# A hybrid decoder layer on one core: the arithmetic of GpSimd given to VectorE, and eight one-hot comparisons written as one

## The chip, the core and the metric

One NeuronCore of a Trainium2 chip runs the whole kernel. The metric is device time in microseconds (us) of one execution; the kernel before takes 2576.43 us, the median of 3 runs (2575.58 to 2576.53). The program has one instruction queue for each engine: TensorE (PE in the profile; its weight loads are PEld), VectorE (DVE), ScalarE (ACT), GpSimd (POOL) and SyncE (SP), which issues nearly all DMAs. Each queue runs in order; semaphores order the queues against each other.

## The reference: what is computed

The input x is 256 tokens of 2048 features. One layer does, all in float32:

```
h  = RMSNorm(x);  P = h @ W_in                       # 6152 columns, split among two groups of heads
mLSTM group (4 heads of 256): causal conv, q/k, gates, chunkwise matrix memory, norm, output gate
dilated group (8 heads of 128): rotary q/k, three dilated windows merged, norm
x += concat(groups) @ W_out
x += CrossAttention(RMSNorm(x), RMSNorm(mem))        # 4 heads of 512, 256 memory tokens
x += PEER(RMSNorm(x))
out = RMSNorm(x)
```

PEER holds 16384 experts, each one row of `u_tab` and one row of `v_tab`. Per token and for each of 8 heads, a query scores 128 first keys and 128 second keys; the best 16 of each make 256 sums, of which the best 16 are picked, with a softmax over them as gates. The result is the sum over the picks of gate * gelu(u . x) * v.

## The kernel before, in words

**Weights.** Activations stand with features on the 128 partitions and the 256 tokens along the free dimension. All big products go through 400 weight tiles of 128x2048 float32 (1 MB each). A tile is loaded by SP (`wload`, line 97) into one of 3 buffers `wst`. `wsplit` (lines 103 to 113) then makes, for each of its two halves of 1024 columns, a high part `whi` by a cast on ScalarE (line 111) and a low part `wlo = wst - whi` by one subtraction (line 112); 3 buffers of halves hold each. `lin_a` (line 122) goes over the 16 chunks of the contraction: per chunk one matmul of `whi` with 512 columns (line 126; high and low part of the activations side by side) and one of `wlo` with 256 columns (line 127).

**Who subtracts.** The argument `lo_engine` of `wsplit` names the engine of line 112. VectorE has it by default. With "both" the half used last goes to GpSimd (32 tiles of the projections: `w_aqk`, `w_min`, `w_mo`). With `G` both halves go to GpSimd: the 16 tiles of `w_pq` (line 688) and the first 32 of the 128 tiles of `uT` (`u_block`, line 626, called in lines 732 and 781). That makes 128 of 800 halves on GpSimd.

**Other work on GpSimd.** The sums of squares of the norms (`square_into`, line 198: ScalarE squares, GpSimd adds 128x256), eight multiplications with a triangle (line 420), and three of the last sixteen multiplications of the output (line 870).

**The part of the program around the change.** After the output product of the cross attention (tiles of `w_xo`) come:

1. 16 tiles of `w_pq`, two for each PEER head. `pq` (line 692) joins the two halves of a product; a small product with the keys (line 669) gives scores in PSUM, and `top16` (lines 658 to 662) takes the best 16 of 128 in five VectorE operations, for two halves of the tokens. After a head's second tile, `cand` (line 677, one broadcast addition) and another `top16` over 256 follow. Beside them runs `scaled_input`: the norm `rstd_ffn`, then `xs` (line 645) and the parts of `hsc` (line 163), the moving operand of all `uT` tiles.
2. The first `u_block`s. Beside them runs `select_chain`: on VectorE, sixteen times, two operations `eq` over 128x512 (lines 709 and 711) and a reduction (line 713); PE then transposes the result into `selT` (line 727).
3. The other `u_block`s up to the 32nd, with 32 gate groups of 8 tokens between them (`gate_group`, line 740). For each token two one-hot rows are made on VectorE: `ob` (line 748) compares the 128 key numbers `iota` with the token's picked second keys, `oa` (line 749) with the first keys, times the gates. PE multiplies them (line 755), ScalarE copies the result out of PSUM (line 758), and a DMA writes it to DRAM. `oa` and `ob` have 2 buffers each.
4. Four more `u_block`s, and then 128 tiles of `v` (lines 818 and 819) with the last 92 tiles of `uT` between them. These cannot start before all gates are in DRAM, because `coef_half` reads them back by expert.

**What sets the order.** The functions above are generators that yield, and `tick` takes one step of each between two tiles of weights. The framework's scheduler then places the instructions on each queue by its own estimates of their durations and by free buffers; a queue runs what it was given in that order.

Of the kernel before, what the change touches and what calls it, by code (L numbers as in the profile page):

```python
# [20 lines left out]
P = 128  # L21
# [18 lines left out]
# columns of the packed small parameters  # L40
S_GMIX, S_GCROSS, S_GMEM, S_GFFN, S_GFIN = 0, 16, 32, 48, 64
S_CW, S_CB, S_GM, S_GA, S_BI, S_BF, S_N = 80, 112, 120, 128, 136, 137, 138
# columns of the packed constants
# [5 lines left out]
def hybrid_layer(ctx: ExitStack, tc: tile.TileContext, a, out):  # L49
    nc = tc.nc  # L50
    V, S, G, PE = nc.vector, nc.scalar, nc.gpsimd, nc.tensor
# [48 lines left out]
    def wtile(src, lo_engine=None, order=(0, 1)):  # L100
        return wsplit(wload(src), lo_engine, order)

    def wsplit(st, lo_engine=None, order=(0, 1)):
        """the parts of the tile's two halves; lo_engine "both" gives the half used last to GpSimd"""
        parts = {}
        for i in order:
            hi = wp.tile([P, 1024], F32R, tag="whi", name=f"whi{n_w[0]}_{i}", bufs=3)
            lo = wp.tile([P, 1024], F32R, tag="wlo", name=f"wlo{n_w[0]}_{i}", bufs=3)
            eng = (V, G)[i != order[0]] if lo_engine == "both" else lo_engine or V
            src = st[:, i * 1024:(i + 1) * 1024]  # L110
            S.copy(hi, src)  # L111
            eng.tensor_tensor(lo, src, hi.bitcast(F32), op=OP.subtract)  # L112
            parts[i] = hi, lo

        def part(which):
            return lambda at, n=P: parts[at // 1024][which][:, at % 1024:at % 1024 + n]
        return part(0), part(1)
# [4 lines left out]
    def lin_a(ps, hi, lo, mov, kcs=range(KC)):  # L122
        """ps[:, :256] + ps[:, 256:] = W.T @ h; mov(k) holds both parts of h's chunk."""
# [6 lines left out]
    def lin_b(pss2, kg, hi, lo, h):  # L130
        """pss2[tt] += h[:, tt].T @ W for four chunks of the contraction."""
# [10 lines left out]
    def rstd_of(dst, ss, n):  # L142
        """dst = (ss / n + eps) ** -0.5: a first guess from the exponent's bits, three steps of Newton's method"""
# [11 lines left out]
    def split_scaled(dst, k, src, g):  # L155
        """dst[:, k] = both parts of src * g (g per partition)"""
# [15 lines left out]
    def as_column(row, name):  # L172
        """[P, 256] with equal partitions -> [P, 2], tokens on partitions."""
# [8 lines left out]
    def residual_block(pool, ps, n, g_at, acc, nxt, first):  # L182
        """resid += ps; acc += resid ** 2; nxt = both parts of resid * g"""
# [8 lines left out]
    def square_into(pool, acc, x, first, tag):  # L192
        if first:
            S.activation(acc, x, AF.Square)
        else:
            sq = pool.tile([P, T], F32, tag="rsq", name=f"rsq{tag}", bufs=2)
            S.activation(sq, x, AF.Square)  # L197
            G.tensor_tensor(acc, acc, sq, op=OP.add)  # L198

    # ================= projections and the two head groups =================  # L200
    chains = []

    def tick():
        """the next step of every chain of small work, between two tiles of weights"""
# [16 lines left out]
    with tc.tile_pool(name="ph1", bufs=2) as p1:  # L221
# [9 lines left out]
        hm = lambda k: h[:, k, :]  # noqa: E731  # L231
# [17 lines left out]
        def join(dst, ps, tag):  # L249
            """dst = ps[:, :256] + ps[:, 256:]"""  # L250
# [4 lines left out]
        def head_norm(sq_parts, n, name):  # L255
            """rstd over the head's features, on every partition"""
# [9 lines left out]
        def proj_rows(src, dst):  # L266
            """one group of 512 columns, tokens on partitions: dst [P, 2, 512]"""
# [15 lines left out]
        def start_chain():  # L283
# [14 lines left out]
            # log sigmoid(f) = min(f, 0) - ln(1 + exp(-|f|))  # L298
# [67 lines left out]
        for half in range(2):  # L366
            vrow = p1.tile([P, 2, 512], F32, tag="vrow", name=f"av{half}")
            proj_rows(a["w_av"][half], vrow)
            for hh in range(4):
                hd = 4 * half + hh  # L370
                qs = p1.tile([P, 2, T], F32, tag="c32", name=f"qs_{hd}")
                for w in range(2):
                    ps = mm_tile()
                    lin_a(ps, *wtile(a["w_aqk"][2 * hd + w], "both"), hm)
# [6 lines left out]
        rows, ogs = {}, {}  # L381

        def mlstm_in(hd):
            """causal conv on the head's two blocks of channels"""
# [4 lines left out]
            for j in range(2):  # L389
                blk = 2 * hd + j  # L390
                ps = mm_tile()
                lin_a(ps, *wtile(a["w_min"][blk], "both"), hm)
# [13 lines left out]
        def mlstm_chain(hd, c32, wq):  # L406
# [4 lines left out]
            # decay weights exp(a_s - max_t), keys on partitions  # L411
# [4 lines left out]
            for s in range(2):  # L416
# [3 lines left out]
                G.tensor_tensor(dw[:, s, s * P:(s + 1) * P], dw[:, s, s * P:(s + 1) * P], tri, op=OP.mult)  # L420
            yield
            # q, k: [features, tokens]
# [23 lines left out]
            # denominator, on every partition  # L446
# [29 lines left out]
        def output_gate(hd):  # L476
            og = p1.tile([P, 2, T], F32, tag="og", name=f"og_{hd}")
            for j in range(2):
                ps = mm_tile()
                lin_a(ps, *wtile(a["w_mo"][2 * hd + j], "both"), hm)  # L480
# [17 lines left out]
    # ================= cross attention =================  # L498
    with tc.tile_pool(name="ph2", bufs=1) as p2:
# [18 lines left out]
        mm_ = lambda k: mh[:, k, :]  # noqa: E731  # L518
# [10 lines left out]
        cm = lambda k: cat[:, k, :]  # noqa: E731  # L529
        for n in range(KC):  # L530
            ps = mm_tile()
            lin_a(ps, *wtile(a["w_out"][n], None, (1, 0)), cm, list(range(8, KC)) + list(range(8)))
# [52 lines left out]
        xm = lambda k: hc[:, k, :]  # noqa: E731  # L585
# [24 lines left out]
        om = lambda k: ocat[:, k, :]  # noqa: E731  # L610
# [7 lines left out]
    # ================= PEER =================  # L618
    gdram = drp.tile([T // GT, P, NK * GT], F32, name="gdram")
    with tc.tile_pool(name="ph3", bufs=2) as p3:  # L620
        act = p3.tile([P, RING, T], F32, name="act", bufs=1)
        hpm = lambda k: hp[:, k, :]  # noqa: E731
        hs = big("hsc")

        def u_block(b, eng=None):
            ps = mm_tile()
            lin_a(ps, *wtile(a["uT"][b], eng), lambda k: hs[:, k, :])
# [6 lines left out]
        with tc.tile_pool(name="ph3g", bufs=2) as pg:  # L634
            def scaled_input():
                """the normalised input of the experts"""
# [45 lines left out]
            for hd in range(RH):  # L682
                keys = pg.tile([P, 2, NK], F32, tag="keys", name=f"keys{hd}")
                nc.sync.dma_start(keys, a["keysT"][:, 2 * hd:2 * hd + 2, :])
                for pp in range(2):
                    n = 2 * hd + pp
                    ps = mm_tile()
                    lin_a(ps, *wtile(a["w_pq"][n], G), hpm)
# [7 lines left out]
            def select_chain():  # L696
                """keys and gates of the picks, picks on partitions"""
# [34 lines left out]
            while chains:  # L732
                u_block(n_u, G)
# [3 lines left out]
        with tc.tile_pool(name="ph3h", bufs=2) as pg:  # L737
            gst = [None]

            def gate_group(t0):  # L740
                """gates of 8 tokens, [second key, first key] each, into gdram"""
# [3 lines left out]
                ob = pg.tile([P, 8, P], F32, tag="ob", name=f"ob{t0}")  # L745
                for i in range(8):
                    t = t0 + i
                    V.tensor_scalar(ob[:, i, :], iota, selT[:, 1, t:t + 1], None, op0=OP.is_equal)  # L748
# [31 lines left out]
            for b in range(n_u, 2 * EB):  # L780
                u_block(b, G)
# [179 lines left out]
```

## Time and profile before

| | |
|---|---|
| median of the runs | 2576.43 us |
| the profiled execution: first to last instruction (span) | 2554.4 us |
| around the span (median less span) | 22.0 us |
| `w_pq` tiles on PE | from 862.5 us |
| first one-hot row on VectorE | 1073.8 us |
| gate products on PE | 1079.3 to 1292.4 us |
| first matmul of `v` | 1316.3 us |

The profile is of one execution. For each engine it gives busy time, groups of like instructions with their number and mean duration, and the idle time before them with what ended it. A duration on VectorE or PE can reach into the next instruction's, because the engines are pipelined; what an instruction really holds the engine for is read from start to start in the timeline. "Granted clock" (PEclk) is the share of TensorE's full speed that was granted.

### The profile page before, as it was taken

The page shows a single profiled execution, that of the slowest core. Times are in us where ns is not written, and L with a number is a line of the kernel's source. Part 1 is how long each engine was busy: PE and PEld are TensorE (multiplying, and loading weights), DVE is VectorE, ACT ScalarE, POOL GpSimd, SP SyncE. Part 2 cuts the span into 40 slices and gives each one's busy share as a digit, 9 for nine tenths or more (in the row PEclk, how much of TensorE's full clock was granted, in tenths as well). Part 3 has the DMA queues.
Part 4 walks back from the last instruction along what each step waited for, and adds up shares of the span by engine and source line. Part 5 has one row for each costly group of instructions (what it writes and reads, how often), then busy time and mean ns, then how long its engine had stood idle before and what let it go on. Part 6 is the DMA issues. An engine that isn't in the chain of part 4 may idle for free.

```text
span 2554.4 us, 34778 instructions
## 1 busy us (share of the span) xinstructions
PE 2436.9 (95%) x13610; PEld 2117.2 (83%) x13610; DVE 1724.6 (68%) x2818; ACT 1202.1 (47%) x1649; POOL 401.6 (16%) x214
## 2 busy tenths in 40 slices
PE   7989999999999879788899999999999999999997
PEld 6777788888888768677888888888888888888886
DVE  6877758744456699899975555655655655556565
ACT  6555446444445434355554444444444444444343
POOL 3131313100001457545400000000000000000001
PEclk9999999999999989899999999999999999999998
DMA  6344435544544434344485656555655565555553
GB/s 244 140 144 148 139 125 205 191 168 173 175 176 169 166 119 162 128 167 184 183 289 213 211 188 208 204 194 202 209 203 184 212 212 200 197 184 183 196 198 116
DMA packets 98710, 466.78 MB, mean 183 GB/s; under 512 B 7537, under 2 KB 41585, under 8 KB 45297
## 3 DMA queue, kind: packets, MB, share of 16 engines
q1 hardware_dynamic: 96096, 447.71, 49.4%
q10 hardware_dynamic: 2448, 16.85, 1.6%
q8 instruction: 107, 1.75, 0.3%
q14 instruction: 59, 0.48, 0.1%
HBM read 445.65 MB, written 18.87 MB: 182 GB/s over the span
## 4 chain that ended last, share of the span: by engine, by line
PE 50%; DVE 14%; issue 1%; POOL 0%; DMA 0%; ACT 0%; DVEq 0%; POOLq 0%; SPq 0%; ACTq 0%
PE sm L818 16%; PE mm L126 15%; PE sm L819 8%; PE mm L127 8%; DVE ob L748 4%; DVE oa L749 4%; PE mm L818 2%; PE mm L819 1%; DVE cand L677 1%; DVE xs L645 0%; POOL wlo L112 0%; DVE hsc L163 0%; DVE eq L711 0%; DVE ut L630 0%; DVE eq L709 0%
## 5 line engine op out<-in xcount | busy, mean ns | idle before, releaser
L112 DVE TENSOR_TENSOR wlo<-wst,whi 128x1024 fp32r<-128x1024 f32 x672 | 825.5, 1230 | 692.0 <-ACT whi L111 689.3
L111 ACT CAST whi<-wst 128x1024 fp32r<-128x1024 f32 x800 | 834.2, 1049 | 937.5 <-PE mm L126 531.0
L126 PE MATMUL mm<-hsc,whi 128*128 128x512 f32 x2048 | 734.2, 400 | 4.1 <-ACT whi L111 4.1
L818 PE MATMUL sm<-coef,whi 128*128 128x512 f32 x1792 | 624.7, 391 | 0.0
L127 PE MATMUL mm<-hsc,wlo 128*128 128x256 f32 x2048 | 581.4, 284 | 9.9 <-POOL wlo L112 8.4
L819 PE MATMUL sm<-coef,wlo 128*128 128x256 f32 x1792 | 500.6, 280 | 0.0
L126 PEld LDWEIGHTS mm<-hsc,whi 128*128 128x128 f32 x2048 | 391.5, 191 | 91.5 <-ACT whi L111 5.0
L127 PEld LDWEIGHTS mm<-hsc,wlo 128*128 128x128 f32 x2048 | 395.1, 193 | 12.2 <-POOL wlo L112 10.3
L818 PEld LDWEIGHTS sm<-coef,whi 128*128 128x128 f32 x1792 | 335.2, 187 | 74.0
L112 POOL TENSOR_TENSOR wlo<-wst,whi 128x1024 fp32r<-128x1024 f32 x128 | 315.6, 2473 | 403.0 <-ACT whi L111 382.3
L819 PEld LDWEIGHTS sm<-coef,wlo 128*128 128x128 f32 x1792 | 338.3, 189 | 0.1
L198 POOL TENSOR_TENSOR facc<-facc,rsqf 128x256 f32<-128x256 f32 x11 | 11.9, 1084 | 1224.2 <-ACT rsqf L197 1224.0
L126 PE MATMUL mm<-h,whi 128*128 128x512 f32 x512 | 187.0, 407 | 0.0
L631 ACT ACTIVATE act<-ut 128x256 f32<-128x256 f32 x128 | 53.6, 419 | 216.3 <-DVE ut L630 216.3
L127 PE MATMUL mm<-h,wlo 128*128 128x256 f32 x512 | 145.4, 284 | 4.3 <-DVE wlo L112 4.0
L748 DVE TENSOR_SCALAR ob<-con,selT 128x128 f32<-128x128 f32 x256 | 127.1, 496 | 6.8 <-PE sm L727 6.8
L749 DVE TENSOR_SCALAR oa<-con,selT 128x128 f32<-128x128 f32 x256 | 119.4, 466 | 0.0
L126 PEld LDWEIGHTS mm<-h,whi 128*128 128x128 f32 x512 | 97.8, 191 | 22.8 <-issue 0.3
L198 POOL TENSOR_TENSOR acc<-acc,rsqr 128x256 f32<-128x256 f32 x30 | 39.2, 1308 | 430.1 <-ACT rsqr L197 425.5
L127 PEld LDWEIGHTS mm<-h,wlo 128*128 128x128 f32 x512 | 98.4, 192 | 6.8 <-DVE wlo L112 5.3
L126 PE MATMUL mm<-hp,whi 128*128 128x512 f32 x256 | 97.6, 420 | 3.3 <-DVE hp L158 3.3
L126 PE MATMUL mm<-ocat,whi 128*128 128x512 f32 x256 | 90.5, 399 | 0.0
(309 smaller groups left out, 3375.6 us busy)
## 6 DMA issues: line engine op xcount, KB each, us to landing
wst<-in_uT SPq DMA_DIRECT2D x128, 1024.0 KB, 4.8
wst<-in_v SPq DMA_DIRECT2D x128, 1024.0 KB, 4.8
wst<-in_w_aqk SPq DMA_DIRECT2D x16, 1024.0 KB, 4.8
wst<-in_w_out SPq DMA_DIRECT2D x16, 1024.0 KB, 4.8
wst<-in_w_xk SPq DMA_DIRECT2D x16, 1024.0 KB, 4.8
wst<-in_w_xq SPq DMA_DIRECT2D x16, 1024.0 KB, 4.8
wst<-in_w_xv SPq DMA_DIRECT2D x16, 1024.0 KB, 4.8
wst<-in_w_xo SPq DMA_DIRECT2D x16, 1024.0 KB, 4.8
```

The lines of the kernel that those rows point to most:

```text
L111: S.copy(hi, src)
L112: eng.tensor_tensor(lo, src, hi.bitcast(F32), op=OP.subtract)
L126: PE.matmul(ps, hi(k * P), mov(k), start=(n == 0), stop=False)
L127: PE.matmul(ps[:, 256:], lo(k * P), mov(k)[:, :256], start=False, stop=(n == len(kcs) - 1))
L198: G.tensor_tensor(acc, acc, sq, op=OP.add)
L631: S.activation(act[:, b % RING, :], tmp, AF.Gelu)
L677: V.tensor_tensor(cand, ts[:, tt, hd, 0, :, None].to_broadcast([P, TK, TK]), ts[:, tt, hd, 1, None, :].to_broadcast([P, TK, TK]), op=OP.add)
L748: V.tensor_scalar(ob[:, i, :], iota, selT[:, 1, t:t + 1], None, op0=OP.is_equal)
L749: V.tensor_scalar(oa[:, i, :], iota, selT[:, 0, t:t + 1], selT[:, 2, t:t + 1], op0=OP.is_equal, op1=OP.mult)
L818: PE.matmul(ps, hi(at), coef[:, c, :], start=(c == 0), stop=False)
L819: PE.matmul(ps[:, 256:], lo(at), coef[:, c, :256], start=False, stop=(c == EB - 1))
```

## The change

`G` is gone from the kernel. Line 112 is always on VectorE, so are the additions of line 198, the triangle and the last multiplications. In `gate_group`, the eight comparisons for `ob` are one VectorE instruction over 128x1024, in which both operands are broadcast; the eight for `oa` stay. The comments and docstrings are gone too, so that line numbers in the new kernel are lower by one between lines 110 and 744.

```diff
-    V, S, G, PE = nc.vector, nc.scalar, nc.gpsimd, nc.tensor
+    V, S, PE = nc.vector, nc.scalar, nc.tensor
...
-    def wsplit(st, lo_engine=None, order=(0, 1)):
+    def wsplit(st, order=(0, 1)):
...
-            eng = (V, G)[i != order[0]] if lo_engine == "both" else lo_engine or V
             src = st[:, i * 1024:(i + 1) * 1024]
             S.copy(hi, src)
-            eng.tensor_tensor(lo, src, hi.bitcast(F32), op=OP.subtract)
+            V.tensor_tensor(lo, src, hi.bitcast(F32), op=OP.subtract)
...
             S.activation(sq, x, AF.Square)
-            G.tensor_tensor(acc, acc, sq, op=OP.add)
+            V.tensor_tensor(acc, acc, sq, op=OP.add)
...
-                    lin_a(ps, *wtile(a["w_aqk"][2 * hd + w], "both"), hm)
+                    lin_a(ps, *wtile(a["w_aqk"][2 * hd + w]), hm)
...
-                G.tensor_tensor(dw[:, s, s * P:(s + 1) * P], dw[:, s, s * P:(s + 1) * P], tri, op=OP.mult)
+                V.tensor_tensor(dw[:, s, s * P:(s + 1) * P], dw[:, s, s * P:(s + 1) * P], tri, op=OP.mult)
...
-                    lin_a(ps, *wtile(a["w_pq"][n], G), hpm)
+                    lin_a(ps, *wtile(a["w_pq"][n]), hpm)
...
-                u_block(n_u, G)
+                u_block(n_u)
...
                 ob = pg.tile([P, 8, P], F32, tag="ob", name=f"ob{t0}")
+                V.tensor_tensor(ob, iota[:, None, :].to_broadcast([P, 8, P]),
+                                selT[:, 1, t0:t0 + 8, None].to_broadcast([P, 8, P]), op=OP.is_equal)
                 for i in range(8):
                     t = t0 + i
-                    V.tensor_scalar(ob[:, i, :], iota, selT[:, 1, t:t + 1], None, op0=OP.is_equal)
                     V.tensor_scalar(oa[:, i, :], iota, selT[:, 0, t:t + 1], selT[:, 2, t:t + 1],
                                     op0=OP.is_equal, op1=OP.mult)
...
-                        (G if i == 3 else V).tensor_tensor(o[:, i, :], resid[:, k, :], fin, op=OP.mult)
+                        V.tensor_tensor(o[:, i, :], resid[:, k, :], fin, op=OP.mult)
```

The two calls with "both" for `w_min` and `w_mo`, and the second call of `u_block` with `G`, change in the same way. How the instructions stand on the queues, before and now, is shown at three places.

The first is VectorE's queue in part 1 above, from the joining of the third `w_pq` product (`pq2`) on. Before:

```order
L692 TENSOR_TENSOR pq2_7360<-mm229_7317,pqt2_7361 128x256
L179 COPY col_ffn_7367<-sm230_7364 128x1 x2
L658 MAX ts_7181<-sm231_7370 128x8
L163 TENSOR_TENSOR hsc_7176<-xs0_7448,hsc_7176 128x256
L659 MAX_INDEX ti_7182<-ts_7181,sm231_7370 128x8
```

Now, at the same place (`wlo133` is the low part of the fourth `w_pq` tile, `_0` and `_1` its halves):

```order
L111 TENSOR_TENSOR wlo133_0_7405<-wst133_7402,whi133_0_7404 128x1024
L691 TENSOR_TENSOR pq2_7360<-mm229_7317,pqt2_7361 128x256
L178 COPY col_ffn_7367<-sm230_7364 128x1 x2
L657 MAX ts_7181<-sm231_7370 128x8
L111 TENSOR_TENSOR wlo133_1_7409<-wst133_7402,whi133_1_7408 128x1024
L658 MAX_INDEX ti_7182<-ts_7181,sm231_7370 128x8
```

The two subtractions of a `w_pq` tile stand between the picks now; the next tile's two (`wlo134`) come 39 rows further on, behind a head's picks and four rows each of `xs` and `hsc`.

The second is VectorE's queue in part 3, around the joining `ut18` of the 19th `u_block`. Before:

```order
L748 TENSOR_SCALAR ob96_9785<-con_74,selT_7177 128x128
L749 TENSOR_SCALAR oa96_9784<-con_74,selT_7177 128x128
L630 TENSOR_TENSOR ut18_9766<-mm301_9723,ut18_9766 128x256
L748 TENSOR_SCALAR ob104_9803<-con_74,selT_7177 128x128
L749 TENSOR_SCALAR oa104_9802<-con_74,selT_7177 128x128
```

Now (`ob104` is the group of 8 tokens from token 104 on; `wlo166` belongs to the 21st `u_block`, two tiles on from the one that `ut18` joins):

```order
L111 TENSOR_TENSOR wlo165_1_9742<-wst165_9735,whi165_1_9741 128x1024
L111 TENSOR_TENSOR wlo166_0_9810<-wst166_9807,whi166_0_9809 128x1024
L629 TENSOR_TENSOR ut18_9682<-mm301_9639,ut18_9682 128x256
L745 TENSOR_TENSOR ob104_9712<-con_74,selT_7177 128x1024
L749 TENSOR_SCALAR oa104_9711<-con_74,selT_7177 128x128 x8
L745 TENSOR_TENSOR ob112_9796<-con_74,selT_7177 128x1024
L749 TENSOR_SCALAR oa112_9795<-con_74,selT_7177 128x128 x8
L111 TENSOR_TENSOR wlo166_1_9814<-wst166_9807,whi166_1_9813 128x1024
```

A group takes nine instructions in place of sixteen, and the low parts stand in the same queue, one and a half to two tiles ahead of their use.

The third is PE's queue where the gate products begin. Before, they stand behind the last matmul of the 11th `u_block` (`whi156`):

```order
L126 MATMUL mm271_8988<-hsc_7176,whi156_1_8995 128x512
L127 MATMUL mm271_8988<-hsc_7176,wlo156_1_8996 128x256
L755 MATMUL sm272_9072<-oa0_9036,ob0_9037 128x128 x4
L755 MATMUL sm273_9078<-oa0_9036,ob0_9037 128x128 x4
L126 MATMUL mm274_9084<-hsc_7176,whi157_0_9087 128x512
```

Now they stand in the middle of the second half of the 12th:

```order
L126 MATMUL mm274_9070<-hsc_7176,wlo157_1_9078 128x256
L125 MATMUL mm274_9070<-hsc_7176,whi157_1_9077 128x512
L755 MATMUL sm272_9058<-oa0_9036,ob0_9037 128x128 x4
L755 MATMUL sm273_9064<-oa0_9036,ob0_9037 128x128 x4
L126 MATMUL mm274_9070<-hsc_7176,wlo157_1_9078 128x256
```

So about one and a half `u_block`s more stand ahead of the first gate product than before, and as many fewer behind it.

More of the change, by code (lines that the diff above doesn't have):

```diff
@@ L98, in wload, with wtile @@
         return st
-    def wtile(src, lo_engine=None, order=(0, 1)):
-        return wsplit(wload(src), lo_engine, order)
-    def wsplit(st, lo_engine=None, order=(0, 1)):
+    def wtile(src, order=(0, 1)):
+        return wsplit(wload(src), order)
+    def wsplit(st, order=(0, 1)):
         parts = {}
@@ L391, in mlstm_in @@
                 ps = mm_tile()
-                lin_a(ps, *wtile(a["w_min"][blk], "both"), hm)
+                lin_a(ps, *wtile(a["w_min"][blk]), hm)
                 xin = p1.tile([P, T + 3], F32, tag="xin", name=f"xin_{blk}")
@@ L479, in output_gate @@
                 ps = mm_tile()
-                lin_a(ps, *wtile(a["w_mo"][2 * hd + j], "both"), hm)
+                lin_a(ps, *wtile(a["w_mo"][2 * hd + j]), hm)
                 join(og[:, j, :], ps, f"o{hd}{j}")
@@ L531, in hybrid_layer @@
             ps = mm_tile()
-            lin_a(ps, *wtile(a["w_out"][n], None, (1, 0)), cm, list(range(8, KC)) + list(range(8)))
+            lin_a(ps, *wtile(a["w_out"][n], (1, 0)), cm, list(range(8, KC)) + list(range(8)))
             residual_block(p2, ps, n, S_GCROSS, acc, hc, n == 0)
@@ L623, in hybrid_layer, with u_block @@
         hs = big("hsc")
-        def u_block(b, eng=None):
+        def u_block(b):
             ps = mm_tile()
-            lin_a(ps, *wtile(a["uT"][b], eng), lambda k: hs[:, k, :])
+            lin_a(ps, *wtile(a["uT"][b]), lambda k: hs[:, k, :])
             tmp = p3.tile([P, T], F32, tag="ut", name=f"ut{b}")
@@ L780, in hybrid_layer @@
             for b in range(n_u, 2 * EB):
-                u_block(b, G)
+                u_block(b)
                 while n_g < (b + 1 - g0) * 32 // (2 * EB - g0):
```

## The prediction

> **What bounds the kernel now.** First the page: the span, and the engines' shares.
>
> ```profile
> span 2554.4 us, 34778 instructions
> PE 2436.9 (95%) x13610; PEld 2117.2 (83%) x13610; DVE 1724.6 (68%) x2818; ACT 1202.1 (47%) x1649; POOL 401.6 (16%) x214
> ```
>
> PE looks like the bound, but these are averages over the program. So second, the busy time by stretches (after the length: PE, PEld, DVE, ACT, POOL, then the granted clock). The third row is the stage of the `w_pq` tiles and the choice of the picks, up to the first one-hot row; I call it A. The fourth is the stage of the gates, up to the first `v` matmul: B.
>
> ```profile
> 60.00:300.00 240.00, 222.63 (x1150) 187.64 (x1148) 183.08 (x312) 121.01 (x199) 60.84 (x28) 0.98 0.41 143
> 380.00:480.00 100.00, 96.12 (x541) 82.25 (x540) 85.70 (x130) 64.24 (x117) 32.33 (x29) 1.00 0.56 200
> 862.50:1073.80 211.30, 172.91 (x909) 148.04 (x908) 189.43 (x541) 78.33 (x115) 132.05 (x54) 0.89 0.38 135
> 1073.80:1316.30 242.50, 217.09 (x1344) 194.12 (x1344) 233.27 (x554) 133.82 (x173) 101.78 (x42) 0.95 0.52 191
> 1500.00:2000.00 500.00, 500.00 (x2886) 440.90 (x2885) 288.91 (x334) 224.78 (x280) 0.00 (x0) 1.00 0.58 202
> ```
>
> From 1500 to 2000 PE never stops, at full clock, with GpSimd idle: nothing is to be had there, and the change touches nothing there. In A and B, 454 us together, VectorE is the busiest (90% and 96%), PE waits, and its clock drops to 0.89 and 0.95. Third, whom PE waited for from 862.5 to 1316.3:
>
> ```profile
> PE sm L755 <- DVE oa L749: 23.9, 12, 3.4
> PE sm L669 <- DVE pq L692: 13.7, 3, 7.1
> PE mm L127 <- POOL wlo L112: 8.4, 6, 2.4
> ```
>
> Mostly VectorE. Fourth, the timeline of VectorE in B, and of GpSimd there:
>
> ```profile
> 1202.11 2.45 DVE L748 TENSOR_SCALAR ob<-con,selT 128x128 f32<-128x128 f32 x1
> 1204.48 0.34 DVE L749 TENSOR_SCALAR oa<-con,selT 128x128 f32<-128x128 f32 x1
> 1204.74 0.28 DVE L748 TENSOR_SCALAR ob<-con,selT 128x128 f32<-128x128 f32 x1
> 1204.93 0.34 DVE L749 TENSOR_SCALAR oa<-con,selT 128x128 f32<-128x128 f32 x1
> 1205.19 0.41 DVE L630 TENSOR_TENSOR ut<-mm,ut 128x256 f32<-128x256 f32 x1
> ```
> ```profile
> 1199.73 4.75 POOL L112 TENSOR_TENSOR wlo<-wst,whi 128x1024 fp32r<-128x1024 f32 x2 [3.48 <-ACT whi L111]
> ```
>
> This is the point on which all rests. The same comparison takes 0.28 us, or 2.45 us when a GpSimd subtraction runs beside it; the long one ends just when GpSimd's second does (1199.73 + 4.75 = 1204.48). VectorE is not working then, it is held up by GpSimd. Its "busy" in A and B is partly a wait.
>
> **Stage A, part by part.** The groups of A that show it, and what GpSimd did there:
>
> ```profile
> L711 DVE TENSOR_TENSOR eq<-eq,tif 128x512 f32<-128x512 f32 x16 | 21.3, 1330 | 0.3
> L677 DVE TENSOR_TENSOR cand<-ts 128x256 f32<-128x256 f32 x16 | 18.3, 1146 | 0.0
> L709 DVE TENSOR_TENSOR eq<-pf,con 128x512 f32<-128x512 f32 x16 | 17.9, 1120 | 0.3
> L645 DVE SCALAR_TENSOR_TENSOR xs<-resid,small,rstd_ffn 128x256 f32<-128x256 f32 x16 | 14.2, 910 | 0.0
> L163 DVE TENSOR_TENSOR hsc<-xs,hsc 128x256 fp32r<-128x256 f32 x16 | 11.8, 759 | 0.0
> L112 POOL TENSOR_TENSOR wlo<-wst,whi 128x1024 fp32r<-128x1024 f32 x53 | 131.4, 2488 | 78.6 <-ACT whi L111 78.6
> ```
>
> Undisturbed ones beside them, and a `wlo` on VectorE followed at once by other work:
>
> ```profile
> 1062.14 0.69 DVE L709 TENSOR_TENSOR eq<-pf,con 128x512 f32<-128x512 f32 x1
> 929.77 0.47 DVE L645 SCALAR_TENSOR_TENSOR xs<-resid,small,rstd_ffn 128x256 f32<-128x256 f32 x1
> 855.22 1.22 DVE L112 TENSOR_TENSOR wlo<-wst,whi 128x1024 fp32r<-128x1024 f32 x1 [0.82 <-ACT whi L111]
> 856.36 0.96 DVE L158 SCALAR_TENSOR_TENSOR hp<-resid,small,hp 128x256 fp32r<-128x256 f32 x1
> ```
>
> Hold-ups removed: `eq` 16 x (1.33 - 0.69) + 16 x (1.12 - 0.69) = 17.1 us; `cand` and `hsc`, which have the size of `ut` above (0.41), 16 x (1.15 - 0.41) + 16 x (0.76 - 0.41) = 17.4; `xs` 16 x (0.91 - 0.47) = 7.0. Together 41.5 us; smaller groups have some too, and I take 45. The upper bound is GpSimd's whole 132 us. Added: 53 subtractions, each of which holds VectorE for 856.36 - 855.22 = 1.14 us: 60.4 us. So VectorE's work goes from 189.4 to 205 us, and with the 21.9 us for which it had nothing to do before (211.3 - 189.4) A would last 227. Some of that idle time went to waits on GpSimd's last sum, so I take 222: **A becomes 11 us longer.** Bounds: 205 (no idle time) and 231 (41.5 removed, all idle time kept), so 6 us shorter to 20 longer. PE's work in A is 26 tiles, and stays below that; a tile is worked out next.
>
> **Stage B.** Its groups on VectorE, GpSimd and PE, two gate products, and what follows them:
>
> ```profile
> L748 DVE TENSOR_SCALAR ob<-con,selT 128x128 f32<-128x128 f32 x256 | 127.1, 496 | 6.8 <-PE sm L727 6.8
> L749 DVE TENSOR_SCALAR oa<-con,selT 128x128 f32<-128x128 f32 x256 | 119.4, 466 | 0.0
> L112 POOL TENSOR_TENSOR wlo<-wst,whi 128x1024 fp32r<-128x1024 f32 x42 | 101.8, 2435 | 107.8 <-ACT whi L111 94.9 <-PE sm L755 13.0
> L126 PE MATMUL mm<-hsc,whi 128*128 128x512 f32 x416 | 157.6, 418 | 0.0
> L755 PE MATMUL sm<-oa,ob 128*128 128x128 f32 x512 | 65.9, 281 | 23.9 <-DVE oa L749 23.9
> ```
> ```profile
> 1110.43 1.95 PE L755 MATMUL sm<-oa,ob 128*128 128x128 f32 x16
> 1112.13 0.48 PE L126 MATMUL mm<-hsc,whi 128*128 128x512 f32 x1
> ```
>
> Undisturbed, an `ob` holds VectorE for 1204.93 - 1204.74 = 0.19 us and an `oa` for 1205.19 - 1204.93 = 0.26. The one `ob` of a group is as large as a `wlo`, so 1.14 us by that row; `eq` of line 709, broadcast in the same way, bounds it: 0.69 for half the size, 1.38 for the whole if nothing is gained by size. I take 1.14. A group is then 1.14 + 8 x 0.26 = 3.2 us where its sixteen instructions take 8 x 0.45 = 3.6 undisturbed: 0.4 x 32 = 12 us less, no more; the hold-ups are the larger part. By their means, `ob` and `oa` lose 256 x (0.496 - 0.28) + 256 x (0.466 - 0.34) = 88 us.
>
> The Trainium skill's page "VectorE: DVE Perf Modes" speaks against the one comparison: its section on the TRN2 errata gives a VectorE operation 58 cycles at 0.96 GHz and its elements over the rate, and its tier table gives float32 comparisons with a scalar two elements a cycle and two-tensor operations one. By that, eight small ones would take 1.02 us and the large one 1.13, an estimate from that page; the 12 us would be a loss of 3.5, and the row of 0.19 us speaks against it.
>
> VectorE in B now: 32 x 3.2 = 102 us, 42 + 9 subtractions at 1.14 (9 are there already, for the last tiles) = 58, `ut` 26 x 0.41 = 11: 171 us. PE in B: the stretch from 1500 to 2000 holds 2886 matmuls, 32 to a tile, so a tile is 5.54 us; the order puts one and a half of the 26 tiles (416 / 16) ahead of the gates, and 24.5 x 5.54 = 135.7. The gates are 32 groups of 16 matmuls at 1112.13 - 1110.43 = 1.70 us: 54.4. So 190 us, more than VectorE's 171: **the bound of B passes from VectorE to PE.** The first group comes ahead of all that (3.2 us), and for waits I leave a quarter of the 23.9 us above, 6: B becomes 199, **43 us shorter** than 242.5. Bounds: 193 without waits; with all the old waits of 23.9, 217, so 49 to 25 shorter. The tile and a half moved into A cost nothing there as long as VectorE is the bound.
>
> **The rest.** In the projections the waits of PE were
>
> ```profile
> PE sm L330 <- DVE qs L326: 10.1, 5, 2.7
> PE sm L348 <- DVE sc L344: 4.9, 4, 1.9
> ```
>
> VectorE loses hold-ups there and gets the subtractions: about as much (28 operations of GpSimd, 60.8 us, for 28 x 1.14 = 32 us). It is 76% busy. I take 4 us of the 15 as gained; between 10 gained and 5 lost. The sums of squares (71 additions of 0.41 us) come where VectorE has room: from 380 to 480, 29 of them add 12 us to 85.7 of 100, and there the neighbours of 0.96 us, as `hp` above, go back to 0.47. The last multiplications: nothing to speak of.
>
> **Sum.** Of the profiled execution: 2554.4 + 11 - 43 - 4 = 2518.4 us of span. The median of the runs lies 2576.4 - 2554.4 = 22.0 us above it, outside the span, which I leave as it is: **2540 us.**
>
> **Rivals.** *The clock (slower).* In A the subtractions of a tile now stand behind a head's picks, so PE's waits get longer and come at each tile. After a wait PE is slow:
>
> ```profile
> 950.98 0.63 PE L126 MATMUL mm<-hp,whi 128*128 128x512 f32 x1
> 951.62 0.63 PE L126 MATMUL mm<-hp,whi 128*128 128x512 f32 x1
> ```
>
> A pair of matmuls takes 0.64 us, a tile 16 x 0.64 = 10.2 in place of 5.54. If VectorE in turn waits for each of the 16 `w_pq` tiles at that rate, A grows by another 16 x 4.7 = 75 us, and the kernel takes 2540 + 75 = 2615. It decides from 36 / 4.7 = 8 such tiles on. For it: the clock of 0.89 in A. Against it: PE's work in A, 16 x 10.2 + 10 x 5.54 = 219 us even then, fits beside VectorE's 222. 8%. By the Trainium skill's page "TensorE: Matmul & The Clock Gate", Part 1, the clock falls to a half after an idle window of about 3.4 us and is back after one as long; by that each wait would cost 1.7 us, 27 in all, and the time would be 2567, not slower.
>
> *VectorE paces B still.* The copies, the DMA of the gates or the two buffers of `oa` and `ob` keep the old waits, B gains 25 and A loses 20: 2576.4 - 25 + 20 - 4 = 2567; with nothing gained in the projections and some clock, no change. 18%, of which 6 end within 0.2% of before (what a measurement of this kernel can tell from no change, 5 us).
>
> *All goes well.* A stays as it was or gets shorter, B has no waits, 10 us in the projections: 2576.4 - 0 - 49 - 10 = 2517. 12%.
>
> The forecast has the rest, 62%. That gives faster 0.86 (62, 12 and 12), same 0.06, slower 0.08. The range goes from 2515, the good case, to 2567, where the second rival stands.
>
> **What would show it.** Right: `ob` at about 1.2 us; no `oa`, `eq`, `cand` or `xs` over its undisturbed time; B near 199 us with PE over 95% busy and VectorE near 85%; A near 222 us with VectorE over 90%. Wrong: long VectorE operations that stay with GpSimd idle (then it was not GpSimd); `w_pq` tiles mostly at 0.64 us a pair with VectorE idle (the clock); PE waiting on `oa` as long as before.

## The result, and the profile after

| | before | after |
|---|---|---|
| median of the runs on one chip (4 runs each) | 2576.01 us | 2501.93 us |
| lowest and highest | 2563.85, 2576.53 | 2483.79, 2503.76 |
| span of the profiled execution | 2554.4 us | 2501.8 us |

The ratio is 0.9708, with a 95% interval from 0.9672 to 0.9745. The kernel became 74 us faster, where 36 were forecast: the sign was right, the time lies 13 us below the range. The profiled execution of the changed kernel took 2503.71 us, only 1.9 us more than its span.

The page of the changed kernel, span and engines:

```profile
span 2501.8 us, 34366 instructions
PE 2435.9 (97%) x13610; PEld 2106.6 (84%) x13610; DVE 1677.8 (67%) x2804; ACT 1199.4 (48%) x1647; POOL 0.2 (0%) x4
```

VectorE has 128 subtractions more, 146 us at 1.14, and is busy 47 us less: so a part of its busy time before was waiting. Next the busy time by stretches of the changed kernel (length; PE, PEld, DVE, ACT, POOL; granted clock): the projections, A, B, and the same 500 us of the `v` stage as in the prediction.

```profile
42.50:346.40 303.90, 303.02 (x1595) 256.75 (x1594) 240.38 (x443) 169.64 (x263) 0.00 (x0) 1.00 0.44 156
827.90:1045.20 217.30, 183.01 (x955) 153.64 (x954) 196.74 (x601) 84.38 (x121) 0.00 (x0) 0.91 0.40 139
1045.20:1244.90 199.70, 196.74 (x1298) 178.56 (x1298) 174.18 (x368) 128.80 (x165) 0.00 (x0) 0.99 0.62 226
1500.00:2000.00 500.00, 500.00 (x2832) 433.65 (x2832) 287.64 (x332) 222.11 (x278) 0.00 (x0) 1.00 0.56 197
```

In the projections and in B, PE is now busy for 99.7% and 98.5% of the time; in A VectorE is still the busiest engine, with 91%. Cut at the first instruction of each stage in the timeline, the two profiled executions compare so (us):

| | start | projections | `w_out` to `w_xo` | A | B | `v` | end |
|---|---|---|---|---|---|---|---|
| before | 46.7 | 333.6 | 482.2 | 211.3 | 242.5 | 1220.3 | 17.8 |
| after | 42.5 | 303.9 | 481.5 | 217.3 | 199.7 | 1240.2 | 16.7 |
| change | -4.2 | -29.7 | -0.7 | +6.0 | -42.8 | +19.9 | -1.1 |
| forecast | 0 | -4 | 0 | +11 | -43 | 0 | 0 |

Two entries are far from the forecast: the projections, and the `v` stage, where nothing was changed. The groups of the changed kernel that the prediction named, in A and then in B, and three rows of VectorE's timeline in B:

```profile
L710 DVE TENSOR_TENSOR eq<-eq,tif 128x512 f32<-128x512 f32 x16 | 11.0, 686 | 0.1
L676 DVE TENSOR_TENSOR cand<-ts 128x256 f32<-128x256 f32 x16 | 6.6, 414 | 0.0
L644 DVE SCALAR_TENSOR_TENSOR xs<-resid,small,rstd_ffn 128x256 f32<-128x256 f32 x16 | 7.1, 472 | 0.0
...
L749 DVE TENSOR_SCALAR oa<-con,selT 128x128 f32<-128x128 f32 x256 | 68.4, 342 | 0.0
L745 DVE TENSOR_TENSOR ob<-con,selT 128x1024 f32<-128x1024 f32 x32 | 39.0, 1218 | 0.0
```
```profile
1059.52 1.23 DVE L745 TENSOR_TENSOR ob<-con,selT 128x1024 f32<-128x1024 f32 x1
1060.66 0.42 DVE L629 TENSOR_TENSOR ut<-mm,ut 128x256 f32<-128x256 f32 x1
1061.00 2.13 DVE L749 TENSOR_SCALAR oa<-con,selT 128x128 f32<-128x128 f32 x8
```

Every group stands at its undisturbed duration: `eq` 0.69 us (it was 1.33), `cand` 0.41 (1.15), `xs` 0.47 (0.91), `oa` 0.34 (0.47). An `ob` of eight tokens holds VectorE for 1060.66 - 1059.52 = 1.14 us, the forecast to the digit. Whom PE waits for in the changed kernel: the only rows over 0.3 us of the projections, the longest of A, and the only one over 1 us of B.

```profile
PE mm L126 <- DVE wlo L111: 0.5, 1, 0.5
...
PE mm L126 <- DVE wlo L111: 23.4, 11, 6.0
PE mm L125 <- ACT whi L110: 6.4, 8, 1.1
...
PE mm L126 <- DVE wlo L111: 3.0, 2, 2.3
```

The waits for `qs` and `sc` are gone from the projections, those for `oa` from B. In A, PE waits for low parts that stand behind picks, as the order had shown.

### The profile page after: what moved, and what is told of

The parts are those of the page before. It is cut to its first block, busy times and chain, and to the rows that moved or that the text cites. A ratio compares the mean times of both kernels' runs of the same rounds, so it can differ in the third digit from the quotient of the medians.

```text
span 2501.8 us, 34366 instructions
## 1 busy us (share of the span) xinstructions
PE 2435.9 (97%) x13610; PEld 2106.6 (84%) x13610; DVE 1677.8 (67%) x2804; ACT 1199.4 (48%) x1647; POOL 0.2 (0%) x4
## 4 chain that ended last, share of the span: by engine, by line
PE 58%; DVE 3%; issue 0%; ACT 0%; DVEq 0%; ACTq 0%
PE mm L125 18%; PE sm L818 17%; PE mm L126 9%; PE sm L819 8%; PE mm L818 2%; PE sm L755 2%; PE mm L819 1%; DVE wlo L111 1%; DVE oa L749 0%; DVE ob L745 0%; DVE eq L710 0%; DVE eq L708 0%; DVE sel L712 0%; DVE act L870 0%; DVE ut L629 0%
## 5 line engine op out<-in xcount | busy, mean ns | idle before, releaser
L111 DVE TENSOR_TENSOR wlo<-wst,whi 128x1024 fp32r<-128x1024 f32 x800 | 977.4, 1223 | 715.6 <-ACT whi L110 711.7
L110 ACT CAST whi<-wst 128x1024 fp32r<-128x1024 f32 x800 | 836.1, 1049 | 1026.6 <-PE mm L125 583.8
L818 PE MATMUL sm<-coef,whi 128*128 128x512 f32 x1792 | 634.9, 398 | 0.0
L126 PEld LDWEIGHTS mm<-hsc,wlo 128*128 128x128 f32 x2048 | 388.9, 190 | 10.4 <-DVE wlo L111 10.3
L126 PE MATMUL mm<-hp,wlo 128*128 128x256 f32 x256 | 77.1, 304 | 17.8 <-DVE wlo L111 17.7
L125 PE MATMUL mm<-cat,whi 128*128 128x512 f32 x256 | 91.6, 401 | 0.0
L125 PE MATMUL mm<-mh,whi 128*128 128x512 f32 x256 | 90.4, 398 | 0.0
L125 PE MATMUL mm<-hc,whi 128*128 128x512 f32 x256 | 89.4, 395 | 0.0
L818 PE MATMUL mm<-coef,whi 128*128 128x512 f32 x256 | 88.9, 391 | 0.0
```

What stands on the lines that cost most here:

```text
L111: V.tensor_tensor(lo, src, hi.bitcast(F32), op=OP.subtract)
L125: PE.matmul(ps, hi(k * P), mov(k), start=(n == 0), stop=False)
L126: PE.matmul(ps[:, 256:], lo(k * P), mov(k)[:, :256], start=False, stop=(n == len(kcs) - 1))
L818: PE.matmul(ps, hi(at), coef[:, c, :], start=(c == 0), stop=False)
```

## The experiments

Stage times of every profiled execution, cut in the same way (us). They tell more than the medians, since the `v` stage alone differs by 23 us between executions.

| | start | projections | `w_out` to `w_xo` | A | B | `v` | end |
|---|---|---|---|---|---|---|---|
| 1 before again | 46.8 | 330.4 | 480.0 | 213.1 | 241.7 | 1240.3 | 17.9 |
| 2 after again | 42.5 | 304.4 | 483.6 | 216.8 | 196.9 | 1243.5 | 16.7 |
| 3 GpSimd beside the projections | 42.5 | 353.2 | 484.9 | 218.5 | 199.1 | 1240.2 | 16.7 |
| 4 projections on VectorE | 46.1 | 303.1 | 479.7 | 213.8 | 242.0 | 1223.6 | 17.8 |
| 5 A and B on VectorE | 46.1 | 336.9 | 480.5 | 218.2 | 205.3 | 1220.2 | 17.9 |
| 6 eight comparisons | 42.5 | 303.7 | 481.4 | 218.0 | 206.2 | 1240.2 | 16.7 |
| 7 one comparison alone | 46.7 | 330.6 | 481.8 | 211.4 | 226.3 | 1240.2 | 17.9 |
| 8 sums on GpSimd | 46.0 | 304.2 | 481.4 | 217.7 | 197.5 | 1243.5 | 16.8 |
| 9 GpSimd on constants | 42.9 | 354.8 | 483.0 | 216.2 | 196.8 | 1240.2 | 16.7 |
| 10 half a tile ahead | 43.0 | 304.4 | 483.2 | 209.8 | 198.3 | 1243.5 | 16.7 |

**1 and 2. Both kernels again, unchanged.** The `v` stage had become longer, and the forecast had put 22 us outside the span of before.

> The kernel before, unchanged. Theory P (PE's pace differs from one execution to the next, whatever the kernel: a pair of matmuls took 347 ns in the profile before and 353 to 361 ns in the profile after from 1300 to 2250 us): every run's span lies within 3 us of its time, and times are spread between 2555 and 2577 us, with the pair at 347 ns or above 350 ns in the profile accordingly. Rival (some 22 us lie outside the span, as the prediction took it): a span near 2554 us beside a time near 2576 us.

> The changed kernel, unchanged. Theory P: time 2482 to 2504 us, the span within 3 us of it; in the profile the stages up to the first matmul of v (1245 us) stay within 5 us of the first profile, and the stage of v takes 1220 us at 347 ns a pair or 1240 us at more. Rival: the pace belongs to the program, so the pair is above 350 ns from 1300 to 2250 us again, and never is in the kernel before.

Measured: before 2565.32 us (10 runs, 2556.05 to 2580.01; ratio 0.9984, 0.9950 to 1.0018), after 2502.86 (4 runs, 2482.01 to 2506.66; ratio 0.9695, 0.9630 to 0.9760). The second profile of the kernel before has a span of 2570.2 us, and its run took 2571.98. The stretch of the `v` stage in it:

```profile
1500.00:2000.00 500.00, 500.00 (x2833) 433.65 (x2832) 284.22 (x329) 219.66 (x274) 0.00 (x0) 1.00 0.57 198
```

The same program, with PE always busy at granted clock 1.00, issued 2833 matmuls in 500 us where its first profile had 2886: 1.8% fewer, as many as the changed kernel's 2832. From start to start, a pair of `whi` and `wlo` matmuls takes 353 ns on average between 1400 and 2200 us in one execution and 347 in the other. So the kernel before shows the longer `v` stage too: the +19.9 us are no effect of the change, and the 22 us were not outside the span. That profile was of one of the quicker executions.

**3. One unread GpSimd subtraction beside each projection tile.** VectorE and PE keep the changed kernel's queues: in the traces PE's order is the same throughout, and VectorE's but for one `wlo` that changes place with its neighbour.

```diff
             V.tensor_tensor(lo, src, hi.bitcast(F32), op=OP.subtract)
+            if beside and i == 1:
+                spare = beside.tile([P, 1024], F32, tag="spare", name=f"spare{n_w[0]}", bufs=1)
+                G.tensor_tensor(spare, src, hi.bitcast(F32), op=OP.subtract)
```

> The changed kernel, with one GpSimd subtraction over 128x1024 added for each of the 32 tiles of the projections, where the kernel before had its own; its result goes to a buffer that nobody reads, and PE's and VectorE's queues are the same, instruction by instruction. Theory H (hold-ups: a running GpSimd operation stops VectorE, and PE's waits in the projections come from that): the stage from the first w_av product to the first w_out product grows from 304 us by 15 to 30, and so does the time, to about 2517 to 2534 us; qs and sc show operations over 1.5 us again. Theory O (order: the new order of PE's queue, in which the small products stand later, took the waits away): the time stays within 5 us of the changed kernel's.

Measured: 2552.12 us (8 runs, 2533.24 to 2557.55; ratio 0.9917, 0.9881 to 0.9953). The projections, by the stretch, and PE's two longest waits there:

```profile
42.50:395.70 353.20, 320.87 (x1595) 268.60 (x1594) 288.74 (x442) 169.88 (x263) 101.97 (x32) 0.95 0.38 133
```
```profile
PE sm L332 <- DVE qs L328: 16.1, 6, 4.8
PE mm L129 <- DVE wlo L111: 8.0, 5, 2.9
```

They take 49 us longer, and the waits for `qs` are back, with 32 operations of GpSimd that no one uses. All else stays within 3.4 us. Theory O falls, and the size is past H's 15 to 30 us as well. One doubt was left: the subtraction also keeps the weight buffers. Experiment 9 takes it up.

**4. Only the projections' subtractions to VectorE.** The kernel before without "both", in three places:

```diff
-                    lin_a(ps, *wtile(a["w_aqk"][2 * hd + w], "both"), hm)
+                    lin_a(ps, *wtile(a["w_aqk"][2 * hd + w]), hm)
```

> The kernel before, with the 32 halves of the projections' tiles subtracted on VectorE and nothing else changed; PE's order in the projections is that of the changed kernel, but for one product at the start. Theory H: the projections take about 304 us in place of 334, the rest stays, time 2576 - 30 = 2546 us. If the sums of squares on GpSimd (they stay there) hold VectorE up as much as the subtractions, less than 15 us are gained: over 2561 us.

Measured: 2538.28 us (4 runs, 2523.58 to 2548.31; ratio 0.9865, 0.9796 to 0.9934).

```profile
46.10:349.20 303.10, 302.67 (x1595) 256.76 (x1594) 238.80 (x433) 168.04 (x260) 5.06 (x8) 1.00 0.44 157
```

303.1 us as in the changed kernel, with B as before (242.0): these 32 subtractions are the whole of the 30 us. The eight multiplications that stay on GpSimd there (5.06 us) do no visible harm.

**5. Only the subtractions of A and B to VectorE.** The sixteen comparisons stay:

```diff
-                    lin_a(ps, *wtile(a["w_pq"][n], G), hpm)
+                    lin_a(ps, *wtile(a["w_pq"][n]), hpm)
...
-                u_block(n_u, G)
+                u_block(n_u)
...
-                u_block(b, G)
+                u_block(b)
```

> The kernel before, with the low parts of the w_pq tiles and of the first 32 uT tiles on VectorE; the projections, the sums and the eight comparisons of a group are those of before. Theory H (the gain of B is that GpSimd no longer holds VectorE up): stage A 212 to 222 us (it was 211 and 214 in the two kernels whose subtractions there were GpSimd's, 217 where they are VectorE's), stage B 199 to 206 us where it was 242, since VectorE's own work there, 171 + 12 us, stays below PE's 190; the projections stay at 330 to 335 us; the time 30 to 40 us below the kernel before. Rival C (the one broadcast comparison made B shorter): B stays above 215 us and the time falls by less than 25 us.

Measured: 2536.78 us (4 runs, 2526.85 to 2547.72; before beside it 2575.32; ratio 0.9870, 0.9806 to 0.9934). A 218.2 and B 205.3, both in H's intervals, and the time is 38.5 us below the kernel before; the projections, put at 330 to 335, took 336.9. Of B's 43 us, 37 come from GpSimd alone.

**6. The changed kernel with eight comparisons again.**

```diff
-                V.tensor_tensor(ob, iota[:, None, :].to_broadcast([P, 8, P]),
-                                selT[:, 1, t0:t0 + 8, None].to_broadcast([P, 8, P]), op=OP.is_equal)
...
+                    V.tensor_scalar(ob[:, i, :], iota, selT[:, 1, t:t + 1], None, op0=OP.is_equal)
```

> The changed kernel with the eight comparisons of a token group put back in place of the broadcast one. By the row of 0.19 us each, VectorE gets 12 us more in B (174 to 186 us) and stays below PE's 197: B 199 to 203 us, the time within 5 us of the changed kernel (2498 to 2508). By the Trainium skill's figures for the two forms VectorE gets 3.5 us less, and B stays at 199 to 200. Rival C: VectorE's 12 us are waited for, since oa and ob have two buffers: B 208 to 215 us.

Measured: 2512.90 us (4 runs, 2510.50 to 2515.30; ratio 0.9766, 0.9710 to 0.9823). Its B, and PE's wait there:

```profile
1045.60:1251.80 206.20, 199.54 (x1299) 179.05 (x1298) 187.63 (x593) 127.99 (x165) 0.00 (x0) 0.99 0.60 218
```
```profile
PE mm L126 <- DVE wlo L111: 6.6, 7, 3.1
```

VectorE is busy 187.63 - 174.18 = 13.5 us more, near the 12 of the row, so the figures of the Trainium skill's page "VectorE: DVE Perf Modes", its section on the TRN2 errata, do not hold here: by an estimate from them it would have been 3.5 less. But B is 6.5 us longer, between the two expectations, and the time is past the 2498 to 2508 expected: VectorE at 91% is not wholly hidden behind PE. (The five profiles with the B of the changed kernel have it between 196.8 and 199.7 us, so it may be up to 9.) A low part that is late now and then makes PE wait (3.6 us more), and PE is busier by 2.8.

**7. One comparison, with GpSimd as before.** The edit of 6, reversed, in the kernel before.

> The kernel before with the one broadcast comparison alone; GpSimd keeps its subtractions. Theory H1 (VectorE stands still for nearly as long as GpSimd subtracts, whatever it has to run: 88 of 102 us in B): VectorE saves its own 12 us and no more, B 225 to 235 us where it was 242, the time 5 to 18 us below the kernel before. Rival H2 (each short VectorE operation that meets a subtraction loses a fixed time, so that fewer and longer ones lose less): B 200 to 215 us, the time 27 to 42 us below.

Measured: 2551.66 us (10 runs, 2542.81 to 2567.31; ratio 0.9929, 0.9889 to 0.9969). Its B, and VectorE's two groups there:

```profile
1070.50:1296.80 226.30, 212.95 (x1344) 191.31 (x1343) 211.45 (x330) 132.31 (x173) 103.51 (x42) 0.96 0.55 205
```
```profile
L750 DVE TENSOR_SCALAR oa<-con,selT 128x128 f32<-128x128 f32 x256 | 139.8, 614 | 0.0
L746 DVE TENSOR_TENSOR ob<-con,selT 128x1024 f32<-128x1024 f32 x32 | 48.7, 1523 | 7.3 <-PE sm L727 6.8
```

H1 holds by the stage: B is 226.3, 16 us shorter. The medians are 24 us apart, outside H1's 5 to 18, but the times of both kernels fall into two groups (means 2545 and 2564 here, 2561 and 2580 before), and group by group they are 16 to 17 us apart. The hold-ups moved to `oa`, whose mean went from 466 ns to 614. They are 256 x (0.614 - 0.342) + 32 x (1.523 - 1.218) = 79 us beside GpSimd's 103.5, as against 88 beside 101.8 before: VectorE loses by the time that GpSimd runs, not by the number of its own operations.

**8. The changed kernel with the sums of squares on GpSimd.**

```diff
-            V.tensor_tensor(acc, acc, sq, op=OP.add)
+            G.tensor_tensor(acc, acc, sq, op=OP.add)
```

> The changed kernel with the sums of squares of the residual blocks back on GpSimd; nothing else runs there. Theory: the sums were worth nothing, because they come where PE is the bound: every stage within 2 us of the changed kernel, the time within 5 us of it. Rival: VectorE's neighbours go from 0.47 to 0.96 us beside them and PE waits for a residual block: the stage of w_out and cross attention gets 5 to 15 us longer.

Measured: 2497.60 us (4 runs, 2488.29 to 2508.89; ratio 0.9692, 0.9626 to 0.9758), no different from the changed kernel. The start alone is longer, 46.0 us in place of 42.5, at a granted clock of 0.93 in its first 46 us where the changed kernel's had 1.00:

```profile
0.00:46.00 46.00, 35.24 (x132) 26.94 (x133) 30.31 (x57) 29.61 (x57) 13.74 (x19) 0.93 0.74 273
```

So the sums are worth 3.5 us, all at the start, more than the 2 us that the theory allowed a stage, and nothing in the stage of `w_out`, the only one that the forecast had looked at.

**9. GpSimd busy with constants.** As 3, but the subtraction reads no weights; one copied column of the high part starts it.

```diff
+                G.tensor_copy(spare[:, :1], hi.bitcast(F32)[:, :1])
+                G.tensor_tensor(spare, con1[:, :1024], con1[:, 640:1664], op=OP.subtract)
```

> The changed kernel with, beside each of the 32 projection tiles, one GpSimd subtraction of 1024 columns that reads only constants and writes a buffer that nobody reads; a copy of one column of the tile's high part starts it. It keeps no buffer of the weights, as the subtraction of the kernel with GpSimd beside the projections did (49 us longer there). Theory H (GpSimd's running alone holds VectorE up, and PE waits for the operation that is held): the projections 325 to 350 us where they were 304, with PE waiting for qs and sc again, the time 20 to 46 us above the changed kernel. Rival K (those 49 us came from weight buffers that GpSimd kept): projections 303 to 312 us.

Measured: 2555.32 us (9 runs, 2540.81 to 2560.67; ratio 0.9904, 0.9873 to 0.9936). Its projections by the stretch, and PE's waits:

```profile
42.90:397.70 354.80, 321.77 (x1596) 269.52 (x1594) 289.10 (x441) 169.75 (x263) 110.12 (x63) 0.95 0.37 132
```
```profile
PE sm L333 <- DVE qs L329: 13.4, 4, 4.4
PE sm L351 <- DVE sc L347: 9.2, 3, 4.8
PE mm L130 <- DVE wlo L111: 9.0, 6, 3.4
```

51 us longer, though all that GpSimd reads of the weights is a copied column, 0.94 us on average: K falls, and GpSimd's running is the cause. Again the size is above what was expected, 325 to 350 us.

**10. The first half of each next tile split ahead of the picks, in A.** The same instructions in another order; two helpers split a tile in two steps:

```diff
+    def wfirst(src):
+        st, parts = wload(src), {}
+        wparts(parts, st, (0,))
+        return parts, st
...
-                    lin_a(ps, *wtile(a["w_pq"][n]), hpm)
+                    lin_a(ps, *wrest(ahead), hpm)
...
+                    ahead = wfirst(a["w_pq"][n + 1] if n < 2 * RH - 1 else a["uT"][0])
                     chains.append(pick_chain(hd, pp, q, keys))
                     tick()
```

> The changed kernel with the split of the first half of each next tile issued ahead of the picks of the tile before it, in A only; same instructions, another order on ScalarE and VectorE. Theory Q (A is longer than VectorE's 197 us because PE waits 23 us for low parts that stand behind picks, and runs slowly after each): A 200 to 212 us where it was 217, PE's waits for wlo there below 12 us, the time 5 to 17 us below the changed kernel. Rival V (VectorE's work and its own waits set A, whatever the order): A 215 to 219, the time within 5 us of the changed kernel.

Measured: 2479.86 us (6 runs, 2473.11 to 2501.00; before beside it 2579.86; ratio 0.9619, 0.9577 to 0.9662), the lowest median of the study. Its interval overlaps the second one of the changed kernel (0.9630 to 0.9760), and four of its six runs lie near 2477 and two near 2500; so what is shown of its gain is what the stages show: up to the `v` stage it is 6.2 us ahead of the changed kernel. Its A, and PE's longest wait there:

```profile
830.60:1040.40 209.80, 179.59 (x975) 151.71 (x974) 197.06 (x602) 85.19 (x122) 0.00 (x0) 0.94 0.41 146
```
```profile
PE mm L140 <- DVE wlo L115: 25.7, 14, 5.7
```

A is 7.5 us shorter (216.2 to 218.5 in the six profiles with the changed kernel's A), in Q's interval, but not for Q's reason: PE waits for low parts as long as before (25.7 us, 23.4 in the changed kernel). VectorE has the same work, 197 us, and its time without work went from 217.3 - 196.7 = 20.6 us to 12.7. VectorE is still the busiest engine of A, as V says, but against V the order matters: in this run it changed how long VectorE stands idle.

## Why the prediction was right in kind and too small

**Right: VectorE's busy time was partly a wait.** Experiments 3 and 9 show it directly (GpSimd alone brings the hold-ups and PE's waits back), 7 shows by how much, and every group that was named went to its undisturbed duration.

**Right: B.** Forecast 199 us with PE as the bound, measured 199.7. VectorE's work was put at 171 us (174.2), PE's at 190 (196.7), the first group and the waits at 9.2 (PE was idle for 3.0). The bound is right; that the total fits so closely is luck, since two misses of 6 to 7 us cancel. Experiment 5 gives 37 us of it to GpSimd, 6 the other 6.5 to the one comparison. That VectorE's 12 us for the comparisons would lie hidden in B was half right: 6.5 of 13.5 reach the time.

**Nearly right: A.** Forecast +11, measured +6.0. VectorE is busy 196.7 us, not 205, and without work for 20.6, not 17. The groups that were named gave what was forecast (`eq` 17.3 us, `cand` 11.7); but the small groups lost another 14 us where 3.5 had been taken. PE does wait for low parts behind the picks at a granted clock of 0.91, as the clock rival had it. What that costs is not shown; it can be no more than the 20.6 us for which VectorE had no work, and experiment 10, by its order, took 7.9 of them away.

**Wrong: the projections.** The failed step is "I take 4 us of the 15 as gained; between 10 gained and 5 lost". Measured: 30 (29.7 here; 333.6 - 303.1 = 30.5 in experiment 4), twice all the waits from which the step took its part. The step before it was right: VectorE loses in hold-ups about what it gets in subtractions, 240.7 us busy before and 240.4 after. But from equal work it does not follow that the waits stay. A row of the stretch that the prediction had not asked for holds the whole gain:

```profile
46.70:380.30 333.60, 311.42 (x1595) 261.65 (x1594) 240.74 (x400) 169.82 (x262) 84.89 (x40) 0.98 0.40 142
```

PE had 333.6 - 311.4 = 22.2 us without work, of which the two rows quoted were 15.0, and its 1595 matmuls took 311.4 us where they take 303.0 undisturbed: 8.4 us more. Of these, 6.8 are half of four stretches of 3.4 us at half clock, each behind a wait. Both went to almost nothing, 21.3 + 8.4 = 29.7. One such wait in the kernel before, by stretches of 2 us, and then by GpSimd's, VectorE's and PE's rows in it:

```profile
148.00:150.00 2.00, 0.85 (x6) 0.49 (x4) 1.97 (x3) 1.79 (x3) 1.45 (x1) 1.00 0.43 180
150.00:152.00 2.00, 0.47 (x2) 0.45 (x3) 2.00 (x2) 0.00 (x0) 0.92 (x1) 0.97 0.28 33
152.00:154.00 2.00, 2.00 (x7) 1.64 (x6) 1.62 (x3) 0.00 (x0) 0.00 (x0) 0.50 0.72 250
154.00:156.00 2.00, 2.00 (x9) 1.71 (x9) 0.70 (x2) 0.00 (x0) 0.00 (x0) 0.67 0.57 242
```
```profile
148.55 2.38 POOL L112 TENSOR_TENSOR wlo<-wst,whi 128x1024 fp32r<-128x1024 f32 x1 [3.86 <-PE mm L127]
148.75 2.73 DVE L326 TENSOR_TENSOR qs<-qs,sw 128x512 f32<-128x512 f32 x1
151.53 1.75 PE L330 MATMUL sm<-qs 128*128 128x256 f32 x4 [2.68 <-DVE qs L326]
```

Beside GpSimd's subtraction a `qs` takes 2.73 us in place of 0.69, PE waits 2.68 us for it, and then runs at half clock for over 3 us: a wait can cost more than its row in the view of the waits. The Trainium skill's page "TensorE: Matmul & The Clock Gate", Part 1, lets the clock fall after an idle window of about 3.4 us. Here waits of 1.95 to 2.68 us were enough (at 97, 152, 209 and 315 us), while two others, of 1.98 and 2.15 us (at 183 and 68 us), left the clock at 1.00. The prediction had used that rule for the waits of A alone, and put no price on the clock here.

Most of the waits ended on work that GpSimd had held up. `qs` is one link of a chain from PE over VectorE back to PE. In two of the five waits for it, `qs` itself was long, as above; in the other three it was an operation that stands ahead of it in VectorE's queue (`nt<-nx,hr_a`, 2.6 us in place of 0.42). A subtraction of 1.14 us, by contrast, has room before it is used: for all the low parts of the projections PE waits 0.5 us in the changed kernel. So from equal work on VectorE equal waits do not follow. Two of the groups in the projections of the kernel before, and of the changed kernel:

```profile
L326 DVE TENSOR_TENSOR qs<-qs,sw 128x512 f32<-128x512 f32 x8 | 9.6, 1196 | 0.1
L344 DVE TENSOR_SCALAR sc<-sc,sum 128x256 f32<-128x256 f32 x16 | 7.0, 478 | 0.2
```
```profile
L325 DVE TENSOR_TENSOR qs<-qs,sw 128x512 f32<-128x512 f32 x8 | 5.5, 687 | 0.0
L343 DVE TENSOR_SCALAR sc<-sc,sum 128x256 f32<-128x256 f32 x16 | 4.9, 350 | 0.2
```

**Not in the sum: the start.** The prediction has no term for it. It became 4.2 us shorter, and by experiment 8 the sums of squares are 3.5 of them.

**Wrong in its reason: the 22 us.** "Outside the span, which I leave as it is": a run takes 2 us more than its span (1.8 in experiment 1), and the rest is PE's pace in the `v` stage, which differs between executions. The sum was not hurt: the profiled runs near the medians (2571.98 and 2503.71 us) both have the slower pace. Set against the stages, it comes out: 2540 less 25.7 (projections), 4.2 (start), 5.0 (A) and 1.6 (the rest) is 2503.5, and the profiled run took 2503.7. What sets the pace stays open; no experiment here changed it at will.

**The rivals.** That VectorE still paces B is refuted by B's rows. The clock rival had the place right and the price wrong. "All goes well" came nearest, and it too allowed only 10 us in the projections. The single parts add up: 30.5 (experiment 4), 37.2 less 6.9 (5), 6.5 (6) and 3.5 (8) make 70.8 us, and up to the `v` stage the changed kernel is 71.4 us ahead.

## What to carry to other kernels

Where one engine holds another up, price the delay on the chains that pass through the held operations, not the held engine's total: the work that takes its place may be as long and delay no one. The gain of a wait removed is read from PE's whole stretch, its time without work and its busy time against undisturbed matmuls, since the rows of waits leave out the slow clock behind them. And before a difference between a median and a span is called outside, the same stage should be compared in two executions of the same kernel.

## What the hardware showed that was not expected

**GpSimd holds up some VectorE operations and others not at all.** Beside GpSimd, operations with two operands in SBUF get longer (by the means of their groups, `qs<-qs,sw` 687 to 1196 ns, `cand` 414 to 1146), and so does `tensor_scalar` (`sc` 350 to 478). One whose first operand is in PSUM does not: of the sixteen `pq<-mm,pqt` of A, seven lie wholly beside a GpSimd operation and take 407 to 425 ns, where the mean without GpSimd is 418. Nor does the reduction that follows each pair of `eq` in A (four lie wholly beside GpSimd and take 668 to 686 ns), though the `eq` went from 1330 and 1120 ns to 686 and 685. Before and after:

```profile
L713 DVE TENSOR_REDUCE sel<-eq 128x32 f32<-128x512 f32 x16 | 10.9, 679 | 0.3
L692 DVE TENSOR_TENSOR pq<-mm,pqt 128x256 f32<-128x256 f32 x16 | 6.6, 410 | 3.1 <-ACT pqt L691 3.1
```
```profile
L712 DVE TENSOR_REDUCE sel<-eq 128x32 f32<-128x512 f32 x16 | 10.9, 679 | 0.1
L691 DVE TENSOR_TENSOR pq<-mm,pqt 128x256 f32<-128x256 f32 x16 | 6.7, 418 | 4.2 <-ACT pqt L690 4.1
```

The Trainium skill's page "SBUF — State Buffer", section "Who interferes with whom", states this division: a port pair shared by the two engines, locked for a whole instruction, that VectorE needs for a second SBUF input or a two-port mode. The rows agree. Which operations of a chain are exposed could so have been read from their operands.

**The price of an operation on GpSimd.** 32 of them that nobody uses cost 49 us (experiment 3, GpSimd busy for 102 us) and 51 us (9, 110 us): about half of GpSimd's busy time came out as time of the kernel, in a stage where VectorE had 63 us to spare.

**PE's pace.** 347 or 353 ns for a pair of matmuls at granted clock 1.00. Over the `v` stage, whose work no kernel here changes, that makes 1220 to 1224 us in three of the twelve profiled executions and 1240 to 1244 in nine. It can change within an execution: the changed kernel goes from 353 ns to 347 at 2303 us, behind its last tile of `uT`, so both paces are found in both kernels. VectorE and ScalarE do not share it: between 1400 and 2200 us, `wlo` takes 1224 ns on average and `whi` 1047 to 1049 in both executions of the kernel before.
